# A two-layer decoder trunk: compression products over four column quarters, stick-breaking heads in pairs, heads alternating in the value products

## The chip, the cores and the metric

The kernel runs on one core of one Trainium2 chip. The metric is the device time of one launch in microseconds. A core has a matrix engine (PE in the profile, with its weight loads shown apart as PEld), a vector engine (DVE), a scalar engine (ACT), a third elementwise engine (POOL) and a queue engine (SP) that issues the DMAs of the weights.

## The reference, cut to what matters

Two layers, each `x + 0.5 SwiGLU`, then a mixer, then `x + 0.5 SwiGLU`. SEQ is 256, the model width 1024, all in float32. The mixer runs three attentions over one projection of the normed input and adds them with learned gates. The parts that the change touches:

```
# A, stick-breaking, 4 heads of 64: per head and block of 128 queries
z = q @ k.T / 8
log_1m = where(past, log_sigmoid(-z), 0)
tail = reversed exclusive cumsum of log_1m over keys
w = where(past, exp(log_sigmoid(z) + tail), 0);  o = w @ v
# B, NSA, 8 heads in 2 groups: o = g0*compressed + g1*selected + g2*window
nsa_compress: blocks of 32 tokens, stride 16 -> 15 blocks per group
    silu(flat(blocks + pe) @ w1) @ w2        # w1: 2048 x 128, w2: 128 x 64, for k and for v
# C, DSA, 4 heads: an indexer scores all keys, the top 64 are kept, softmax over them, times v
```

## The kernel before, in words

The weights (some 209 MB) stream through as tiles of 128x1024 (512 KB, four buffers). Each is split into a high part `wh` (line 244, ACT) and a low part `wl` (line 246, DVE, a few on POOL), and the products run as `wh` by the activations and `wl` by their high part. One such tile is a unit. Up to two units are split ahead of the one whose products run (`LA`).

The attention work of a mixer runs in threads (Python generators: `keys`, `indexer`, `queries`, `nsa_units`, `compress`, `stick_breaking`, `nsa`, `compressed`, `dsa`). After each unit, `tick` lets each thread go on to its next `yield n`, which means: be called again n units later. So the program order of PE is units with pieces of attention between them, and PE keeps exactly the written order (`pe` chains each instruction to the one before). The order on DVE, ACT and POOL is set by a tile scheduler from priorities and dependences, and within an engine it is fixed as well. Banks of PSUM are shared by tag: `acc` three, `sc` two, `tp` two, `o` one.

What the change touches:

- `compress` (lines 778 to 837). POOL writes `flat`, the 15 blocks of each group beside each other for k and v. Then four chunks of `w1` (one weight load of 512 KB each) with eight products: the 30 columns of `flat` are the stationary operand, 128 columns of `w1` stream, and all 16 products of k (or v) add up in 30 rows of bank `o`. A plain float32 product is two passes on PE, and the trace has a record for each. Then a sigmoid on 30x256 (exp on ACT, lines 799 to 801 on DVE), two transposes back, copies into `hrep` (line 613), a product with `w2`, a norm and a rotation of the compressed key (lines 816 to 828), `kc` (line 611 on ACT and line 675 on POOL), two transposes of it, and `kC`.
- `sb_head` (lines 1017 to 1046), one thread for each of the four heads, two units apart. Scores z into an `acc` bank, from 64 rows of `qT` and `kT` (a head is the upper or lower half of the 128 rows); Abs (line 1025), exp and ln (line 477) on ACT; line 1028 on DVE adds max(z, 0), line 1030 casts to the high part, line 1032 takes the low part; two units after z, four products with `tri` add the cumulated sum into the same bank; then exp to `w`, and the value products into 64 rows of a `tp` bank.
- `nsa_unit` (lines 963 to 979): the value products of two heads, one into the upper, one into the lower 64 rows of bank `o`: all of the one head, then all of the other. `dsa` (lines 905 on) does the like for four heads.

In names of the order listings, the number behind a name is the buffer's.

Of the kernel before, what the change touches and what calls it, by code (L numbers as in the profile page):

```python
# [17 lines left out]
P = 128  # L18
# [38 lines left out]
def _constants():  # L57
# [30 lines left out]
    put("csc", c)  # L88
    put("snc", s)
    put("rowmask", (r[:, None] // 16 == np.arange(8)[None, :]))  # L90
    cm = np.zeros((P, NT, 16))
# [19 lines left out]
HG = 2  # L111
WB = 4
WARM = 40
# [12 lines left out]
def decoder_trunk(ctx: ExitStack, tc: tile.TileContext, x_in, consts, gains, hgain, gu1, dn1, win, wkc, wgate, cw1, cw2,  # L126
# [339 lines left out]
    def mixer(l, nrm, nxt):  # L466
# [215 lines left out]
        def indexer():  # L682
# [22 lines left out]
            for t in range(NT):  # L705
# [6 lines left out]
                for h0 in range(0, 8, per):  # L712
                    sc = psum("sc", SC).rearrange("p (h k) -> p h k", k=nk)
                    for j in range(per):
                        mm(sc[:, j], iqS[:, h0 + j, t * P:(t + 1) * P], ikS[:, 0:nk], True, True)
                    rl = mt([512], "rl", 2).rearrange("p (h k) -> p h k", k=nk)
                    A.activation(out=rl, in_=sc, func=AF.Relu)
                    for j in range(per):
                        w = iw[:, t, h0 + j:h0 + j + 1]
                        if h0 + j == 0:  # L720
                            V.tensor_scalar(out=isc[t], in0=rl[:, j], scalar1=w, scalar2=None, op0=ALU.mult)
                        else:
                            V.scalar_tensor_tensor(out=isc[t], in0=rl[:, j], scalar=w, in1=isc[t], op0=ALU.mult,  # L723
                                                   op1=ALU.add)
                    if h0 % 4 == 0:
                        yield 1
# [47 lines left out]
        kC = mt([2, 32], "kC", 1, F32R)  # L774
        vpad = mt([8, HD], "vpad")

        def compress():
            yield from need("f")
            yield 2
            flat = b4("flat")[:, 0:64 * NC].rearrange("p (k j g c) -> p k j g c", k=2, j=16, g=2)  # L780
            for kv in range(2):
                for hf in range(2):
                    for g in range(2):
                        fv = fk[:, kv, g, 1:257].rearrange("p (c j e) -> p j c e", j=8, e=2)[:, :, hf:hf + NC, 0]
                        G.tensor_tensor(out=flat[:, kv, 8 * hf:8 * hf + 8, g], in0=fv,
                                        in1=pos[:, kv, 8 * hf:8 * hf + 8].unsqueeze(2).to_broadcast([P, 8, NC]), op=ALU.add)
            hid = psum("o", 1)
            for kv in range(2):
                for c in range(2):
                    w1 = load(cw1[l, kv][:, c * 1024:(c + 1) * 1024])  # L790
                    yield 1
                    for j in range(8):
                        jj = c * 8 + j
                        mm(hid[0:2 * NC, kv * P:(kv + 1) * P], flat[:, kv, jj].rearrange("p g c -> p (g c)"),
                           w1[:, j * P:(j + 1) * P], jj == 0, jj == 15)
            hs = mt([2, P], "kc4")[0:2 * NC]
            hv = hid[0:2 * NC, 0:2 * P].rearrange("p (a b) -> p a b", b=P)
            act_exp(out=hs, in_=hv, scale=-1.0)
            V.tensor_scalar(out=hs, in0=hs, scalar1=1.0, scalar2=None, op0=ALU.add)
            V.reciprocal(out=hs, in_=hs)  # L800
            V.tensor_tensor(out=hs, in0=hs, in1=hv, op=ALU.mult)
            hrep = mt([2, 4, 2, 16], "hrep")
            G.memset(hrep, 0.0)
            yield 2
            tp = psum("tp", TP)
            for kv in range(2):
                pe(T.transpose(tp[:, kv * 32:kv * 32 + 2 * NC], hs[:, kv], ident[0:2 * NC, 0:2 * NC]))
            for kv in range(2):
                evens(out=hrep[:, kv, :, :, 0:NC], in_=tp[:, kv * 32:kv * 32 + 2 * NC]
                              .rearrange("p (g c) -> p g c", c=NC).unsqueeze(1).to_broadcast([P, 4, 2, NC]))  # L810
            yield 2
            c2 = psum("o", 1)
            for kv in range(2):
# [17 lines left out]
            stack_k(kc4, kc.unsqueeze(1), 1)  # L831
            G.tensor_tensor(out=vpad, in0=c2s[:, 1].unsqueeze(1).to_broadcast([P, 8, HD]),
                            in1=cc("rowmask").unsqueeze(2).to_broadcast([P, 8, HD]), op=ALU.mult)
# [67 lines left out]
        def dsa():  # L901
            yield from need("mdsa", "qD")
            for t in range(NT):
# [12 lines left out]
                o = psum("tp", TP)  # L916
                for h in range(4):
                    for b in range(t + 1):
                        mm(o[h % 2 * HD:(h % 2 + 1) * HD, h // 2 * P:(h // 2 + 1) * P], vds[:, b], PT[h][b],
                           b == 0 and h < 2, True)  # L920
# [38 lines left out]
        def nsa_unit(t, i):  # L959
# [13 lines left out]
            yield from need(("o", t), 2)  # L973
            for a in range(2):
                for b in range(t + 1):
                    for j in range(2):
                        mm(ob[t][a * HD:(a + 1) * HD, i * P:(i + 1) * P], (vsel, vwin)[j][:, b, a], PT[2 * a + j][b], False,
                           True)
# [3 lines left out]
        def nsa():  # L982
            yield from need("PTc")
            for t in range(NT):
                ob[t] = o = psum("o", 1)
                for i in range(4):
                    mm(o[:, i * P:(i + 1) * P], vpad[:, 2 * i:2 * i + 2].rearrange("p a d -> p (a d)"),
                       PTc[:, t * P:(t + 1) * P], i == 0, True)
# [16 lines left out]
        def stick_breaking():  # L1005
# [5 lines left out]
            yield 1  # L1011
            for h in range(4):
                spawn(sb_head(h))
                yield 2

        def sb_head(h):
            i, a = h // 2, h % 2
            d = slice(a * HD, (a + 1) * HD)
            z = psum("acc", ACC)
            mm(z[:, 0:S], kT[d, i, 0:P], qT[d, i], True, False)  # L1020
            mm(z[:, S:S + P], kT[d, i, P:S], qT[d, i, P:S], False, False)
            mm(z[:, 0:512].rearrange("p (b q) -> p b q", b=2)[:, :, 0:P], negi, mstr, False, True)
            z = z[:, 0:S + P]
            sp = mt([512], "rl", 2)[:, 0:S + P]
            A.activation(out=sp, in_=z, func=AF.Abs)
            act_exp(out=sp, in_=sp, scale=-1.0)
            act_exp(out=sp, in_=sp, func=AF.Ln, bias=1.0)
            V.scalar_tensor_tensor(out=sp, in0=z, scalar=0.0, in1=sp, op0=ALU.max, op1=ALU.add)
            sh = mt([S + P], "w", WB, F32R)
            V.tensor_copy(out=sh, in_=sp)  # L1030
            sl = mt([S + P], "w", WB, F32R)
            V.tensor_tensor(out=sl, in0=sp, in1=sh.bitcast(F32), op=ALU.subtract)
            yield 2
            for v in (sh, sl):
                mm(z, tri[:, 0], v, False, False)
            for v in (sh, sl):
                mm(z[:, P:S], tri[:, 1], v[:, S:S + P], False, v is sl)
            yield 2
            w = mt([S + P], "w", WB)
            act_exp(out=w, in_=z)  # L1040
            yield 1
            o = psum("tp", TP)
            mm(o[d, 0:S], vsb[:, 0, h * HD:(h + 1) * HD], w[:, 0:S], True, False)
            mm(o[d, P:S], vsb[:, 1, h * HD:(h + 1) * HD], w[:, S:S + P], False, True)
            A.activation(out=OT[0][d, i], in_=o[d, 0:S], func=AF.Copy)
            V.tensor_tensor(out=OT[1][d, i], in0=o[d, 0:S], in1=OT[0][d, i].bitcast(F32), op=ALU.subtract)

# [165 lines left out]
```

## Time and profile before

| | us |
|---|---|
| median of 3 runs (lowest, highest) | 1254.26 (1252.81, 1255.97) |
| the profiled execution | 1254.2 |
| its span in the trace | 1252.2 |
| mean granted clock of PE | 0.993 of full |
| PE busy, share of the span | 1231.1 (98%) |
| DVE busy | 906.6 (72%) |
| ACT busy | 696.9 (56%) |
| POOL busy | 168.8 (13%) |

The profile's page first lists the busy time of each engine. Then comes the chain of work that ended last: from the last instruction back, at each step to what released it, with the share of the span that each engine has in it. A timeline row has the start in us, the duration in us, the engine, the line, the operation, the tiles written and read, the shape, and how many instructions of one kind the row holds; in brackets the idle time ahead of it and what ended that. Matmuls are pipelined, so two neighbouring rows of PE overlap: what a piece of work costs is read from its start to the next row's start. A layer's mixer lies at 206 to 446 us in the first layer and at 820 to 1066 us in the second.

### The profile page before, as it was taken

Reading aid. Unit: us, or ns where it says so; the run is one execution under the profiler, and the core shown is the slowest. Engines: PE = TensorE matmul, PEld = TensorE weight load, DVE = VectorE, ACT = ScalarE, POOL = GpSimd, SP = SyncE. Lnnn points to the kernel's source line nnn. Section 1 sums busy time; section 2 is a strip of 40 time slices with the busy share of each in tenths; the row PEclk is TensorE's granted clock in tenths of the full one; section 3 lists DMA queues with packets and bytes.
Section 4 is the critical chain, followed back from the end, with each engine's and each line's share of the span. In section 5 each row is a group of like instructions: output and inputs, shape, how many; then the busy total and the mean of one; then the engine's idle time right before and its main releaser. Section 6 shows DMA issues by size and latency. Waiting matters only on the chain.

```text
span 1252.2 us, 20870 instructions
## 1 busy us (share of the span) xinstructions
PE 1231.1 (98%) x7868; PEld 1096.9 (88%) x7868; DVE 906.6 (72%) x1592; ACT 696.9 (56%) x1261; POOL 168.8 (13%) x193
## 2 busy tenths in 40 slices
PE   8999999989999999999999999999899999999998
PEld 7888888878999988888888888888798999888887
DVE  6777677898675976666776666779977668777654
ACT  6655554545665565555555555545556745555542
POOL 2211011220001121110111110131200012111100
PEclk8999999989999999999999999999999999999999
DMA  6655565543333565555655555665333345555563
GB/s 232 192 193 188 184 186 188 192 134 110 127 102 118 175 195 186 185 182 184 189 179 192 186 181 185 190 192 187 119 119 109 118 141 183 179 193 191 180 201 107
DMA packets 61171, 212.05 MB, mean 169 GB/s; under 512 B 7024, under 2 KB 8592, under 8 KB 61072
## 3 DMA queue, kind: packets, MB, share of 16 engines
q1 hardware_dynamic: 60480, 209.63, 52.2%
q0 software_dynamic: 448, 1.08, 0.4%
q8 instruction: 61, 1.00, 0.3%
q14 instruction: 38, 0.31, 0.1%
q10 hardware_dynamic: 144, 0.02, 0.0%
HBM read 209.14 MB, written 1.05 MB: 168 GB/s over the span
## 4 chain that ended last, share of the span: by engine, by line
PE 89%; DVE 7%; ACT 1%; issue 1%; DMA 1%; POOL 1%; SPq 0%; DVEq 0%; POOLq 0%; ACTq 0%
PE acc L195 68%; PE sc L195 16%; PE o L195 2%; DVE wl L246 2%; PE tp L664 2%; PE tp L195 1%; ACT wh L244 1%; DVE isc L733 1%; DMA x<-in_x 1%; DVE isc L723 0%; DVE m L732 0%; DMA hg<-in_hgain 0%; POOL v L422 0%; DVE kc L800 0%; POOL kc L675 0%
## 5 line engine op out<-in xcount | busy, mean ns | idle before, releaser
L244 ACT ACTIVATE wh<-raw 128x1024 fp32r<-128x1024 f32 (+3 forms) x405 | 412.2, 1021 | 452.1 <-PE acc L195 309.1
L246 DVE TENSOR_TENSOR wl<-raw,wh 128x1024 fp32r<-128x1024 f32 (+3 forms) x397 | 469.0, 1184 | 244.1 <-ACT wh L244 242.7
L195 PE MATMUL acc<-aT,wh 128*128 128x512 f32 (+1 forms) x1696 | 462.3, 344 | 2.6 <-DVE aT L356 2.6
L195 PE MATMUL acc<-aT,wl 128*128 128x256 f32 x1280 | 361.0, 282 | 0.2 <-DVE wl L246 0.2
L195 PEld LDWEIGHTS acc<-aT,wh 128*128 128x128 f32 x1696 | 292.8, 190 | 45.2 <-DVE aT L356 3.9
L195 PE MATMUL acc<-hT,wh 128*128 128x512 f32 (+1 forms) x792 | 247.9, 369 | 0.0
L195 PEld LDWEIGHTS acc<-aT,wl 128*128 128x128 f32 x1280 | 243.9, 191 | 1.1 <-DVE wl L246 1.0
L195 PE MATMUL acc<-hT,wl 128*128 128x256 f32 x704 | 199.1, 283 | 0.0
L195 PE MATMUL sc<-aT,wh 128*128 128x512 f32 x544 | 192.4, 396 | 0.0
L195 PEld LDWEIGHTS acc<-hT,wh 128*128 128x128 f32 x792 | 142.8, 188 | 26.9
L195 PE MATMUL sc<-aT,wl 128*128 128x256 f32 x544 | 152.5, 280 | 0.6 <-DVE wl L246 0.6
L195 PEld LDWEIGHTS acc<-hT,wl 128*128 128x128 f32 x704 | 132.4, 188 | 0.0
L422 POOL TENSOR_TENSOR v<-v,R 128x256 f32<-128x256 f32 x88 | 69.7, 796 | 415.5 <-DVE v L338 362.9
L195 PEld LDWEIGHTS sc<-aT,wh 128*128 128x128 f32 x544 | 102.0, 188 | 23.8
L195 PE MATMUL acc<-wh,aT 128*128 128x512 f32 (+1 forms) x320 | 108.4, 405 | 0.0
L195 PEld LDWEIGHTS sc<-aT,wl 128*128 128x128 f32 x544 | 102.7, 189 | 0.9 <-DVE wl L246 0.9
L195 PEld LDWEIGHTS acc<-wh,aT 128*128 128x128 f32 x320 | 62.4, 195 | 12.2 <-issue 0.4
L366 POOL TENSOR_TENSOR ssum<-ssum,sq 128x256 f32<-128x256 f32 x42 | 39.4, 938 | 194.5 <-ACT sq L365 194.1
L195 PE MATMUL acc<-wl,aT 128*128 128x512 f32 (+1 forms) x160 | 63.2, 395 | 0.0
L246 POOL TENSOR_TENSOR wl<-raw,wh 128x1024 fp32r<-128x1024 f32 x8 | 19.6, 2452 | 269.6 <-ACT wh L244 269.6
L337 ACT ACTIVATE half<-acc 128x256 f32<-128x256 f32 x136 | 49.4, 365 | 2.6 <-PE acc L195 1.2
L424 DVE TENSOR_TENSOR v<-v,v 128x256 f32<-128x256 f32 x88 | 38.3, 437 | 13.1 <-ACT v L423 5.1
(242 smaller groups left out, 1444.8 us busy)
## 6 DMA issues: line engine op xcount, KB each, us to landing
raw<-in_gu SPq DMA_DIRECT2D x175, 512.0 KB, 4.1
raw<-in_dn SPq DMA_DIRECT2D x64, 512.0 KB, 3.6
raw<-in_wgate SPq DMA_DIRECT2D x48, 512.0 KB, 3.3
raw<-in_win SPq DMA_DIRECT2D x32, 512.0 KB, 3.3
raw<-in_dn SPq DMA_DIRECT2D x32, 384.0 KB, 3.0
raw<-in_wbr SPq DMA_DIRECT2D x16, 512.0 KB, 3.5
raw<-in_wout SPq DMA_DIRECT2D x16, 512.0 KB, 3.4
raw<-in_cw SPq DMA_DIRECT2D x8, 512.0 KB, 4.1
```

Of the source, the lines that this page charges most:

```text
L195: return pe(T.matmul(o, lhsT=lhsT, rhs=rhs, start=start, stop=stop, skip_group_check=True))
L244: A.activation(out=wh[:, w], in_=raw[:, w], func=AF.Copy)
L246: e.tensor_tensor(out=wl[:, w], in0=raw[:, w], in1=wh[:, w].bitcast(F32), op=ALU.subtract)
L337: A.activation(out=t, in_=b[:, S:2 * S], func=AF.Copy)
L366: G.tensor_tensor(out=ssum, in0=ssum, in1=sq, op=ALU.add)
L422: G.tensor_tensor(out=g, in0=g, in1=N["R"], op=ALU.mult)
L424: V.tensor_tensor(out=u, in0=u, in1=g, op=ALU.mult)
L664: pe(T.transpose(tp[:, b * P:(b + 1) * P], src, ident))
L733: V.match_replace(out=isc[t], in_to_replace=m8, in_values=isc[t], imm_value=MARK)
```

## The change: what it does

Three edits.

1. Compression. The 16 products of k (and of v) no longer add up in one place. Each goes to one of four column quarters, 32 wide (30 columns and two spare ones), so product j adds to rows 32·(j mod 4) of the bank. The four sums are then copied by ACT (`hq`), and one product for k and one for v with a constant matrix of zeros and ones ("quarters") adds the four and transposes them at once; they stand where the two transposes stood. The sigmoid is then taken on 128x60 instead of 30x256, and two DVE products write `hrep`. The `yield 2` there becomes a `yield 1`, so the rest of the compression is one unit earlier.
2. Stick-breaking. One thread for two heads, five units apart. The products of z and of o alternate between the two heads (two halves of the rows, two halves of the columns); elementwise work runs on tiles of [2, 384] where it can.
3. In the value products of `nsa_unit` and `dsa` the heads alternate inside the blocks.

The diff, cut to its core:

```diff
@@ compress
-                        mm(hid[0:2 * NC, kv * P:(kv + 1) * P], flat[:, kv, jj].rearrange("p g c -> p (g c)"),
-                           w1[:, j * P:(j + 1) * P], jj == 0, jj == 15)
-            hs = mt([2, P], "kc4")[0:2 * NC]
-            hv = hid[0:2 * NC, 0:2 * P].rearrange("p (a b) -> p a b", b=P)
-            act_exp(out=hs, in_=hv, scale=-1.0)
+                        f0 = (kv * 16 + jj) * 2 * NC
+                        mm(hid[jj % 4 * 32:(jj % 4 + 1) * 32, kv * P:(kv + 1) * P], fl[:, f0:f0 + 32],
+                           w1[:, j * P:(j + 1) * P], jj < 4, jj >= 12)
+            hq = mt([2, P], "kc4")
+            A.activation(out=hq, in_=hid[:, 0:2 * P].rearrange("p (a b) -> p a b", b=P), func=AF.Copy)
+            hrep = mt([2, 4, 2, 16], "hrep")
+            G.memset(hrep, 0.0)
+            yield 1
+            tp = psum("tp", TP)
+            for kv in range(2):
+                mm(tp[:, kv * 2 * NC:(kv + 1) * 2 * NC], hq[:, kv], cc("quarters"), True, True)
+            hs = mt([4 * NC], "hs4")
+            act_exp(out=hs, in_=tp[:, 0:4 * NC], scale=-1.0)
             V.tensor_scalar(out=hs, in0=hs, scalar1=1.0, scalar2=None, op0=ALU.add)
             V.reciprocal(out=hs, in_=hs)
-            V.tensor_tensor(out=hs, in0=hs, in1=hv, op=ALU.mult)
-            hrep = mt([2, 4, 2, 16], "hrep")
-            G.memset(hrep, 0.0)
-            yield 2
-            tp = psum("tp", TP)
             for kv in range(2):
-                pe(T.transpose(tp[:, kv * 32:kv * 32 + 2 * NC], hs[:, kv], ident[0:2 * NC, 0:2 * NC]))
-            for kv in range(2):
-                evens(out=hrep[:, kv, :, :, 0:NC], in_=tp[:, kv * 32:kv * 32 + 2 * NC]
-                              .rearrange("p (g c) -> p g c", c=NC).unsqueeze(1).to_broadcast([P, 4, 2, NC]))
+                a, b = (v[:, kv * 2 * NC:(kv + 1) * 2 * NC].rearrange("p (g c) -> p g c", c=NC).unsqueeze(1)
+                        .to_broadcast([P, 4, 2, NC]) for v in (hs, tp))
+                V.tensor_tensor(out=hrep[:, kv, :, :, 0:NC], in0=b, in1=a, op=ALU.mult)
             yield 2
...
@@ dsa
-                for h in range(4):
-                    for b in range(t + 1):
+                for b in range(t + 1):
+                    for h in range(4):
@@ nsa_unit
-            for a in range(2):
-                for b in range(t + 1):
-                    for j in range(2):
+            for b in range(t + 1):
+                for j in range(2):
+                    for a in range(2):
@@ stick_breaking
-            for h in range(4):
-                spawn(sb_head(h))
-                yield 2
+            for i in range(2):
+                spawn(sb_pair(i))
+                yield 5
+        def sb_pair(i):
+            halves_ = [slice(a * HD, (a + 1) * HD) for a in range(2)]
+            zs = [psum("acc", ACC) for _ in range(2)]
+            for z, d in zip(zs, halves_):
+                mm(z[:, 0:S], kT[d, i, 0:P], qT[d, i], True, False)
+            for z, d in zip(zs, halves_):
+                mm(z[:, S:S + P], kT[d, i, P:S], qT[d, i, P:S], False, False)
...
+            for a in range(2):
+                A.activation(out=sp[:, a], in_=zs[a], func=AF.Abs)
             act_exp(out=sp, in_=sp, scale=-1.0)
             act_exp(out=sp, in_=sp, func=AF.Ln, bias=1.0)
+            for a in range(2):
+                V.scalar_tensor_tensor(out=sp[:, a], in0=zs[a], scalar=0.0, in1=sp[:, a], op0=ALU.max, op1=ALU.add)
+            sh = mt([2, S + P], "w", WB, F32R)
             V.tensor_copy(out=sh, in_=sp)
+            sl = mt([2, S + P], "w", WB, F32R)
             V.tensor_tensor(out=sl, in0=sp, in1=sh.bitcast(F32), op=ALU.subtract)
             yield 2
             for v in (sh, sl):
+                for a in range(2):
+                    mm(zs[a], tri[:, 0], v[:, a], False, False)
...
+            for a in range(2):
+                mm(o[halves_[a], 0:S], v(a, 0), w[:, a, 0:S], True, False)
+            for a in range(2):
+                mm(o[halves_[a], P:S], v(a, 1), w[:, a, S:S + P], False, True)
```

Beside this, `vpad` shares the buffer of `p1`, the tile `rl` is [2, 384] wide, and `w` of stick-breaking lies in it.

How the instructions move. First PE at the scores of stick-breaking in the first layer, before (one head):

```order
L195 MATMUL acc_3442<-qT_2171,kT_2170 128x256
L195 MATMUL acc_3442<-qT_2171,kT_2170 128x128
L195 LDWEIGHTS negi
L195 MATMUL acc_3442<-mstr,negi 128x2x128
L195 MATMUL acc_3461<-aT_132,wh_3330 128x256 x2
```

and after (two heads, in the banks 3444 and 3445):

```order
L196 MATMUL acc_3444<-qT_2170,kT_2169 128x256
L196 MATMUL acc_3445<-qT_2170,kT_2169 128x256
L196 MATMUL acc_3444<-qT_2170,kT_2169 128x128
L196 MATMUL acc_3445<-qT_2170,kT_2169 128x128
L196 LDWEIGHTS negi
L196 MATMUL acc_3444<-mstr,negi 128x2x128
L196 LDWEIGHTS negi
L196 MATMUL acc_3445<-mstr,negi 128x2x128
L196 MATMUL acc_3469<-aT_132,wh_3332 128x256 x2
```

The second head's scores stood two units later before; they now stand between those of the first.

PE at the end of the compression in the first layer, before: `dq` are transposes of another thread, `kc` the compressed key, and the `acc` rows one unit's twelve products of 512 columns.

```order
L664 MATMUL tp_2973<-cst,dq_2870 128x128 x4
L195 MATMUL acc_2959<-wh_2900,aT_132 128x512
L195 MATMUL acc_2959<-wl_2901,aT_132 128x512
L195 MATMUL acc_2959<-wh_2900,aT_132 128x512 x2
L195 MATMUL acc_2959<-wl_2901,aT_132 128x512
L195 MATMUL acc_2959<-wh_2900,aT_132 128x512
L195 MATMUL acc_2960<-wh_2900,aT_132 128x512
L195 MATMUL acc_2960<-wl_2901,aT_132 128x512
L195 MATMUL acc_2960<-wh_2900,aT_132 128x512 x2
L195 MATMUL acc_2960<-wl_2901,aT_132 128x512
L195 MATMUL acc_2960<-wh_2900,aT_132 128x512
L664 MATMUL tp_3021<-cst,kc_577_2949 128x128 x2
```

and after:

```order
L665 MATMUL tp_2975<-cst,dq_2887 128x128 x4
L665 MATMUL tp_2989<-cst,kc_569_2899 128x128 x2
L196 MATMUL acc_2961<-wh_2906,aT_132 128x512
L196 MATMUL acc_2961<-wl_2907,aT_132 128x512
L196 MATMUL acc_2961<-wh_2906,aT_132 128x512 x2
L196 MATMUL acc_2961<-wl_2907,aT_132 128x512
L196 MATMUL acc_2961<-wh_2906,aT_132 128x512
```

The transposes of the compressed key stand one unit (twelve products) earlier.

DVE at the end of the compression in the first layer, before: `c2s` is the compressed key before its transposes, `q`, `ra` and `rb` belong to the query thread, and `m` to the top 64 of the indexer.

```order
L637 SCALAR_TENSOR_TENSOR w_2884<-w_2884,u_2882 128x1
L626 TENSOR_TENSOR rb_2980<-q_402_2154,cst 128x8x8
L638 SCALAR_TENSOR_TENSOR y_2883<-w_2884,y_2883 128x1
L732 MAX m_589_3005<-isc_2377 128x8
L823 SCALAR_TENSOR_TENSOR c2s_2818<-c2s_2818,y_2883,hg_2140 128x64
L628 TENSOR_TENSOR q_402_2154<-ra_2979,rb_2980 128x8x16
L825 TENSOR_TENSOR cra_2892<-c2s_2818,cst 128x16
L826 TENSOR_TENSOR crb_2893<-c2s_2818,cst 128x8
L827 TENSOR_TENSOR crb_2893<-c2s_2818,cst 128x8
L844 CAST q_402_2154<-q_402_2154 128x8x64
L828 TENSOR_TENSOR c2s_2818<-cra_2892,crb_2893 128x16
L246 TENSOR_TENSOR wl_2990<-raw_2987,wh_2989 128x1024
```

and after:

```order
L831 SCALAR_TENSOR_TENSOR c2s_2783<-c2s_2783,y_2825,hg_2140 128x64
L734 MATCH_REPLACE isc_2377<-m_577_2947,isc_2376 128x128
L833 TENSOR_TENSOR cra_2834<-c2s_2783,cst 128x16
L834 TENSOR_TENSOR crb_2835<-c2s_2783,cst 128x8
L835 TENSOR_TENSOR crb_2835<-c2s_2783,cst 128x8
L601 TENSOR_TENSOR gl_2621<-acc_2846,R_2335 128x512
L836 TENSOR_TENSOR c2s_2783<-cra_2834,crb_2835 128x16
L734 MATCH_REPLACE isc_2377<-m_578_2950,isc_2377 128x256
L637 TENSOR_TENSOR w_2892<-y_2891 128x8
L247 TENSOR_TENSOR wl_2958<-raw_2955,wh_2957 128x1024
L638 SCALAR_TENSOR_TENSOR w_2892<-w_2892,u_2890 128x8
L733 MAX m_591_3011<-isc_2376 128x8
```

The whole query chain (its scale, its gain, its rotation and the cast) and one `wl` stood ahead of the last `c2s` and now stand behind it.

## Rows read from the trace of the kernel before

**Rows 1.** The page: busy time by engine, and the chain that ended last.

```profile
PE 1231.1 (98%) x7868; PEld 1096.9 (88%) x7868; DVE 906.6 (72%) x1592; ACT 696.9 (56%) x1261; POOL 168.8 (13%) x193
...
PE 89%; DVE 7%; ACT 1%; issue 1%; DMA 1%; POOL 1%; SPq 0%; DVEq 0%; POOLq 0%; ACTq 0%
```

**Rows 2.** Windows: window, length; busy of PE, PEld, DVE, ACT, POOL; clock; DMA.

```profile
236.00:282.00 46.00, 41.64 (x239) 35.25 (x238) 42.76 (x108) 22.13 (x39) 10.62 (x9) 0.93 0.45 148
...
312.00:397.00 85.00, 85.00 (x695) 78.30 (x695) 53.00 (x102) 54.79 (x118) 2.36 (x1) 1.00 0.38 120
275.00:281.00 6.00, 5.41 (x14) 4.26 (x15) 4.71 (x17) 0.23 (x1) 0.53 (x1) 0.50 0.42 126
```

**Rows 3.** Timeline of PE at one chunk of the compression.

```profile
225.88 1.93 PE L195 MATMUL o<-raw,flat 128*30 128x128 f32 x16
227.75 0.47 PE L195 MATMUL acc<-wh,aT 128*128 128x448 f32 x1
```

**Rows 4.** Timeline of PE: NSA value products, first block of queries, one unit.

```profile
329.21 0.45 PE L195 MATMUL o<-PT,vsel 128*64 128x128 f32 x4
329.48 0.40 PE L195 MATMUL o<-PT,vwin 128*64 128x128 f32 x4
329.80 0.66 PE L664 MATMUL tp<-cst,E 128*128 128x128 f32 x4
```

**Rows 5.** The same, second block of queries, two units (first and last row).

```profile
383.63 0.43 PE L195 MATMUL o<-PT,vsel 128*64 128x128 f32 x2
...
386.13 0.87 PE L664 MATMUL tp<-cst,E 128*128 128x128 f32 x6
```

**Rows 6.** Timeline of PE: scores, sums and values of stick-breaking heads.

```profile
312.80 0.92 PE L195 MATMUL acc<-qT,kT 64*128 64x256 f32 x4
313.65 0.28 PE L195 MATMUL acc<-mstr,negi 128*128 128x256 bf16 x1
...
320.98 0.77 PE L195 MATMUL acc<-w,tri 128*128 128x384 f32 x4
...
335.57 0.86 PE L195 MATMUL tp<-w,vsb 128*64 128x256 f32 x4
336.37 0.50 PE L195 MATMUL acc<-aT,wh 128*128 128x256 f32 x2
```

**Rows 7.** Timelines of ACT and DVE: from that head's scores to its sums.

```profile
313.97 0.49 ACT L1025 ACTIVATE rl<-acc 128x384 f32<-128x384 f32 x1 [0.20 <-PE acc L195]
...
315.72 1.10 ACT L477 ACTIVATE rl<-rl 128x384 f32<-128x384 f32 x2
...
317.08 0.55 DVE L1028 SCALAR_TENSOR_TENSOR rl<-acc,rl 128x384 f32<-128x384 f32 x1
317.67 0.36 DVE L1030 CAST w<-rl 128x384 fp32r<-128x384 f32 x1
...
319.08 0.55 DVE L1032 TENSOR_TENSOR w<-rl,w 128x384 fp32r<-128x384 f32 x1
```

**Rows 8.** Timelines of DVE and PE from the compression's sigmoid to its transposes.

```profile
233.66 1.23 DVE L246 TENSOR_TENSOR wl<-raw,wh 128x1024 fp32r<-128x1024 f32 x1 [0.45 <-ACT wh L244]
...
245.40 1.38 DVE L799 TENSOR_SCALAR kc<-kc 30x256 f32<-30x256 f32 x1
246.81 1.74 DVE L800 RECIPROCAL kc<-kc 30x256 f32<-30x256 f32 x1
...
268.53 0.68 DVE L652 TENSOR_TENSOR q<-q,y 128x512 f32<-128x512 f32 x1
...
272.98 0.42 DVE L844 CAST q<-q 128x512 fp32r<-128x512 f32 x1
273.31 0.17 DVE L828 TENSOR_TENSOR c2s<-cra,crb 128x16 f32<-128x16 f32 x1
...
273.88 0.33 PE L664 MATMUL tp<-cst,kc 128*128 128x128 f32 x1 [1.42 <-ACT kc L611]
275.59 0.47 PE L664 MATMUL tp<-cst,kc 128*128 128x128 f32 x1 [1.38 <-POOL kc L675]
```

## What the change should do to the time

> **What bounds the kernel now.** The first view is the page: PE is busy for 98% of the span and makes 89% of the chain that ended last [rows 1]. So a microsecond that PE no longer works is a microsecond of the span, unless PE then waits for something that was hidden. The second view, busy time by windows, says where that danger is [rows 2]. From 312 to 397 us, where stick-breaking and NSA run, PE is busy for 85.00 of 85.00 us and the others for at most 65% of it: a saving goes straight into the time there. From 236 to 282 us, where the compressed key is made, PE is busy for only 41.64 of 46.00 and DVE for 42.76: the vector engine is nearly full and PE waits for it. The third view, the timelines, gives the price of each piece from its start to the next row's start.
>
> **Compression products.** A chunk of eight products is 16 passes on PE and takes 227.75 − 225.88 = 1.87 us, 0.117 a pass [rows 3]. How four quarters run, this trace does not show; two halves it does: the eight passes of an NSA unit, four to the upper and four to the lower half, take 329.80 − 329.21 = 0.59 us [rows 4], as much as five of the passes above, that is four places and 0.12 of entry and exit. If four quarters share places as two halves do, 16 passes need four places, so 0.59 as well: 1.28 less a chunk, four chunks a layer, 5.1 us a layer. The two products with the constant matrix stand for two transposes; they cost at most two passes more, 0.2. PE alone would gain 4.9 us a layer.
>
> Whether it does is decided by DVE. Its work from the `wl` at 233.66 to the last `c2s` at 273.31 + 0.17 = 273.48 is 39.8 us with hardly a hole [rows 8, 2]. Out go the addition and the reciprocal on 30x256, 1.38 + 1.74 = 3.1; in come the same on 128x60, by 60 of 256 elements in a row 0.7 (an estimate from these two rows). The product and the copy into `hrep` become two products of a like size: nothing. By the order of DVE the query chain and one `wl` no longer stand ahead of the last `c2s`: two multiplications of 0.68, a cast of 0.42 and a `wl` of 1.23 make 3.0 [rows 8], beside smaller ones (the rotation, a MAX and a replacement), about 1 in all. DVE would be done at 273.5 − 3.1 + 0.7 − 3.0 = 268.1, or 267.1 with the small ones. From there to the second transpose it is 275.59 − 273.48 = 2.1 us, most of it POOL's half of `kc`, as before. So the transposes can run at 269.2 to 270.2.
>
> PE was there at 273.88 − 1.42 = 272.5 and waited 1.42 + 1.38 = 2.8 us for both halves of `kc` [rows 8]. Now it is there 4.9 earlier, and one unit of twelve products earlier, since the transposes moved ahead of it. A product of 512 columns takes 6.00 / 14 = 0.43 at a granted clock of 0.50 (the lower of the two levels, 1.2 GHz, that PE had after this wait) [rows 2], so 0.21 at the full one, and twelve 2.6. PE arrives at 265.0 and waits 4 to 5 us: the wait grows. Behind the transposes are now these twelve products. The slow clock after a wait costs half of six microseconds, some 2.7 of the 5.41 busy ones, in both kernels alike. At the same point of the program PE is then ahead by 275.6 − (270.2 + 2.6) = 2.8 us by the large operations alone, 3.8 with the small ones; above stands PE's own 4.9. I take 3.9, the middle of 2.8 and 4.9, and the same in the second layer, whose mixer has the same program: **7.8 us**, with 5.6 and 9.8 as ends. The other limit on the first step, that PE looks ahead over only some passes and so fills fewer than four quarters at a time, lies within these ends, since DVE swallows it first.
>
> **Values of stick-breaking.** One head's products into 64 rows take 336.37 − 335.57 = 0.80 us [rows 6]. Two heads alternate between the halves that rows 4 show running together, so the second costs almost nothing: 0.80 for each of four pairs, **3.2 us**. The gap ahead of such a stretch is not counted; it would come on top.
>
> **Scores.** A head's z from 64 rows takes 313.65 − 312.80 = 0.85 [rows 6]. No row shows two halves of the rows together. If they share places as columns do, 0.85 × 4 = 3.4. If not, two heads need twelve places of 0.117 = 1.4 instead of 1.7, 1.2 in all. I take **3.0**, near the upper end, since the halves of columns [rows 4] are the nearest thing that was measured.
>
> **NSA values.** In the second block of queries two units have 32 passes and take 386.13 − 383.63 = 2.50 us [rows 5]. The heads stand one behind the other there, and the second gets in only when the first is nearly through. Alternating, 16 places of 0.117 and 0.12 make 1.99: 0.51 less, four such stretches (two a layer), **2.0 us**. The first block (0.59 for eight passes) is at four places already and gains nothing; nor does the DSA loop, whose halves alternated before.
>
> *A rule against this reading.* Rows 4 show the four passes with `vsel` of both heads ahead of the last ones with `vwin`, though the program has the first head's `vwin` before the second head's `vsel`. The Trainium skill (TensorE: Matmul & The Clock Gate, Part 3, The mechanism) says that matmuls start and end strictly in program order, without reordering. By that rule the alternation would also help the first block, and the quarters would fill more slowly, which is rival E below; the trace speaks against it.
>
> **The wait added.** A pair's chain is ACT and DVE work between z and the product with `tri`. For one head it is 0.49 + 1.10 + 0.55 + 0.36 + 0.55 = 3.05 us of work and ran from 313.97 to 319.63 among other work, while PE came to `tri` only at 320.98 [rows 7, 6]. For a pair the work is at most 6.1, so without any overlap it ends at 322.7, 1.7 late. Behind the waiting product on PE stand all units that follow, so a wait there is paid in full. But Abs of one head runs beside the exp of others, the double tiles save starts, and PE begins with the high parts (more than 0.77 us for the four products of one head), so that the low part is needed last. Between 0 and 1.7 I take 0.4 for the first pair of a layer, which has the softmax of NSA on ACT beside it, and nothing for the second: **−0.8**. The third `acc` bank is left to the units during a pair; no row of PE shows a wait for a bank in 312 to 397 [rows 2], and I price it at nothing.
>
> **Sum.** 7.8 + 3.2 + 3.0 + 2.0 − 0.8 = 15.2 us. The profiled execution took 1254.2, the median of the runs is 1254.26, so no correction is needed: 1254.2 − 15.2 = **1239.0 us**. With the ends of each term (5.6 to 9.8, 1.2 to 3.4, stalls 0 to 3.4) it goes from 1234 to 1243.6.
>
> **Rivals.**
>
> A: the compression gains nothing. DVE is full, and what PE saves becomes a longer wait for `kc`; or the four quarters run one after the other and the change does not do what it says there. For it: 42.76 of 46 us [rows 2]. Against it: the order moves 3 us of DVE work behind the key. Time: 1239.0 + 7.8 = 1246.8.
>
> E: products run side by side only in the order of the program. The second pass of a product needs the same place as its first, so the eight products of a chunk need nine places, 1.17 us instead of 0.59: 0.58 × 8 = 4.6, of which the share that reaches the end above (7.8 of 10.3) is 3.5. A pair's values and scores need five places for four: 0.20 × 4 + 0.21 × 4 = 1.6. Time: 1239.0 + 5.1 = 1244.1. Rows 4 speak against it.
>
> B: the chain of DVE gets ahead of PE. Then the wait of 2.8 and the slow clock (2.7) vanish and PE's own 4.9 comes whole: 10.4 a layer, 20.8 instead of 7.8: 1226.0. For it: two DVE operations less and a shorter chain. Against it: DVE would have to be 4 to 5 us faster still.
>
> D, slower: the pair's chain holds PE. If the second head's 3.05 us comes wholly on the path at each of the four pairs, and the clock falls after each wait as it did after 275 us (2.7), that is 5.75 × 4 = 23.0, and with the 0.8 counted already 1239.0 + 22.2 = 1261.2. It decides from 4.0 us a pair (16.0 / 4), where it eats all gains. For it: PE came to `tri` only 1.35 us after the chain's end [rows 6, 7]. Against it: ACT has 54.79 and DVE 53.00 busy in 85 us [rows 2].
>
> **Chances.** Forecast 0.60, A 0.16, E 0.07, B 0.10, D 0.04, others 0.03. About 0.3%, 3.8 us, is what can be told from no change. Forecast, B, A and E are faster by more, less 0.03 for tails of A: 0.90. Within it 0.05 (those tails, half of the others), slower 0.05 (D, the rest). The forecast's own range is 1234 to 1244; down to 1229 and up to 1248 it takes in A and E and leaves out B and D.
>
> **What would show it.** Right: the 16 passes of a chunk take about 0.6 us; a pair's values about 0.8 and its scores 0.85 to 1.4; two NSA units in the second block 2.0; PE still waits for `kc`, 4 to 5 us now, and the wait for `tri` stays below 1 us. A: chunk as short, but the wait for `kc` 7 us or more. E: a chunk of 1.2. B: no wait for `kc` and no window of clock 0.50 behind it. D: waits of PE for `w` of 3 us at the pairs. The forecast is wrong where the chunk is short and a new wait of more than 1 us stands at another place in the mixers.

## The result and the profile after

The changed kernel takes 1231.55 us (median of 4 runs, 1230.66 to 1234.24) against 1254.55 (4 runs, 1252.81 to 1255.97): a ratio of 0.982, 95% interval 0.980 to 0.9839. 1239.0 was forecast, with 1229 to 1248 as range. So the direction held, and the gain of 23 us is half as large again as the 15.2 of the sum. The stated range held only at its wide lower end: 1231.55 lies below the forecast's own 1234 to 1244. One of the nine runs of `sig_act_before` took 1488.27 us at a mean granted clock of 0.752 and is left out of its figures below.

The page of the changed kernel answers to [rows 1]; its execution took 1230.66 us, with a span of 1227.8:

```profile
PE 1204.7 (98%) x7872; PEld 1076.2 (88%) x7872; DVE 895.1 (73%) x1580; ACT 694.1 (57%) x1249; POOL 173.1 (14%) x195
...
PE 86%; DVE 9%; DMA 2%; issue 1%; ACT 1%; SPq 0%; POOL 0%; DVEq 0%; ACTq 0%; POOLq 0%
```

PE has 26.4 us less to do, and its share of the span is what it was. The next rows are the timeline of PE in the changed kernel, first layer; they answer to [rows 3 to 6]:

```profile
239.45 0.65 PE L196 MATMUL o<-raw,flat 128*32 128x128 f32 x16
240.02 0.50 PE L196 MATMUL acc<-wh,aT 128*128 128x512 f32 x1
...
323.31 0.44 PE L196 MATMUL o<-PT,vsel 128*64 128x128 f32 x4
323.58 0.39 PE L196 MATMUL o<-PT,vwin 128*64 128x128 f32 x4
323.90 0.66 PE L665 MATMUL tp<-cst,E 128*128 128x128 f32 x4
...
328.06 0.87 PE L196 MATMUL tp<-rl,vsb 128*64 128x256 f32 x8
328.86 0.92 PE L196 MATMUL acc<-qT,kT 64*128 64x256 f32 x8
329.72 0.39 PE L196 MATMUL acc<-mstr,negi 128*128 128x256 bf16 x2
...
374.72 0.44 PE L196 MATMUL o<-PT,vsel 128*64 128x128 f32 x4
...
376.62 0.55 PE L665 MATMUL tp<-cst,E 128*128 128x128 f32 x3
```

From start to next start: a chunk 0.57 us (it was 1.87), two heads' values 0.80 (0.80 for one), two heads' scores 0.86 (0.85 for one), two NSA units of the second block 1.90 (2.50), the unit of the first block 0.59 as before. By these prices the sixteen passes over four quarters take the time of about four places, and halves of the rows run together as halves of the columns do.

Where the time went is read from three places of each layer's mixer that both programs have. The kernel before, timeline of PE:

```profile
225.88 1.93 PE L195 MATMUL o<-raw,flat 128*30 128x128 f32 x16
283.96 0.28 PE L195 MATMUL sc<-mdsa,negi 128*128 128x256 bf16 x1
396.27 0.39 PE L195 MATMUL acc<-iqS,wh 128*128 128x256 f32 x1
846.16 1.93 PE L195 MATMUL o<-raw,flat 128*30 128x128 f32 x16
903.10 0.28 PE L195 MATMUL sc<-mdsa,negi 128*128 128x256 bf16 x1
1015.41 0.39 PE L195 MATMUL acc<-iqS,wh 128*128 128x256 f32 x1
```

and the changed one:

```profile
227.85 0.64 PE L196 MATMUL o<-raw,flat 128*32 128x128 f32 x16
278.32 0.28 PE L196 MATMUL sc<-mdsa,negi 128*128 128x256 bf16 x1
386.48 0.38 PE L196 MATMUL acc<-iqS,wh 128*128 128x256 f32 x1
832.50 0.64 PE L196 MATMUL o<-raw,flat 128*32 128x128 f32 x16
882.95 0.28 PE L196 MATMUL sc<-mdsa,negi 128*128 128x256 bf16 x1
991.09 0.39 PE L196 MATMUL acc<-iqS,wh 128*128 128x256 f32 x1
```

From the first chunk to the indexer's mask the stage took 58.08 and takes 50.47 in the first layer, 56.94 and 50.45 in the second: 7.6 and 6.5 us, **14.1** where 7.8 was forecast. From there to the projection the stick-breaking and NSA stage took 112.31 and takes 108.16, then 112.31 and 108.14: 4.2 us a layer, **8.3** where 7.4 was forecast. Together 22.4. The spans differ by 24.4; the other 2.0 lie in stages that the change does not touch (last section).

The first of these two is where the forecast was off. PE's waits in the first layer's mixer, kernel before, then changed kernel (total, times, longest):

```profile
PE tp L664 <- ACT kc L611: 1.4, 1, 1.4
PE tp L664 <- POOL kc L675: 1.4, 1, 1.4
PE tp L664 <- DVE hrep L613: 0.9, 1, 0.9
...
PE tp L664 <- ACT kSW L759: 0.6, 1, 0.6
```

```profile
PE tp L665 <- ACT wh L245: 1.5, 1, 1.5
PE tp L665 <- ACT qD L770: 1.5, 1, 1.5
PE tp L665 <- POOL kc L676: 0.8, 1, 0.8
...
PE tp L665 <- ACT PT L901: 0.7, 1, 0.7
PE tp L665 <- ACT kSW L760: 0.6, 1, 0.6
```

In the stage of the key 4.3 us of waits before and 4.4 after. (The releasers of the first two are by the profile's last event. The first one ends as DVE has read the `tp` bank into `hrep`, 251.47 + 0.27; the second stands at the transposes of `kc`.) What differs is the clock, in the rows (as [rows 2]) behind the key's transposes, changed kernel, both layers:

```profile
270.00:276.00 6.00, 6.00 (x27) 4.99 (x28) 6.00 (x20) 1.67 (x4) 1.57 (x1) 1.00 0.59 173
876.00:882.00 6.00, 6.00 (x28) 4.99 (x27) 6.00 (x18) 2.12 (x2) 1.58 (x1) 1.00 0.48 158
```

Before, it was 0.50 for six us in the first layer [rows 2] and for three in the second (896 to 899 us, also 0.50). This is one execution of each kernel, and they stand far apart: the mean granted clock of the profiled executions is 0.993 and 0.999, while 48 other runs of the kernel before that list it have 0.992 to 1.000, 0.9962 on the mean, and the changed kernel's other three runs 0.997, 0.995 and 0.997.

### The profile page after: what moved, and what is told of

It is laid out like the page before. It is cut to its first block, busy times and chain, and to the rows that moved or that the text cites. A ratio compares the mean times of both kernels' runs of the same rounds, so it can differ in the third digit from the quotient of the medians.

```text
span 1227.8 us, 20844 instructions
## 1 busy us (share of the span) xinstructions
PE 1204.7 (98%) x7872; PEld 1076.2 (88%) x7872; DVE 895.1 (73%) x1580; ACT 694.1 (57%) x1249; POOL 173.1 (14%) x195
## 4 chain that ended last, share of the span: by engine, by line
PE 86%; DVE 9%; DMA 2%; issue 1%; ACT 1%; SPq 0%; POOL 0%; DVEq 0%; ACTq 0%; POOLq 0%
PE acc L196 65%; PE sc L196 16%; DVE wl L247 4%; PE tp L665 2%; PE o L196 2%; DMA raw<-in_win 1%; PE tp L196 1%; ACT wh L245 1%; DVE isc L734 1%; DVE m L733 1%; DVE isc L724 1%; DMA x<-in_x 1%; DMA hg<-in_hgain 0%; POOL ssum L367 0%; DVE q L656 0%
## 5 line engine op out<-in xcount | busy, mean ns | idle before, releaser
L196 PE MATMUL acc<-wh,aT 128*128 128x512 f32 (+1 forms) x320 | 104.4, 392 | 0.0
```

Source lines behind the costliest of these rows:

```text
L196: return pe(T.matmul(o, lhsT=lhsT, rhs=rhs, start=start, stop=stop, skip_group_check=True))
```

## The experiments

Theory T, read from the two traces: PE's own saving comes through whole in the compression, and the slow clock behind the key is gone as well. Rival R: that stage gives 7.8 as forecast, and the rest comes from the pairs or from the edits acting together. The ratios are to the kernel before on the same chip.

**Each edit alone.** `p1_compress`, `p2_pairs` and `p3_alternate` are the kernel before with one of the three edits of the diff each.

> The kernel before with the compression edit alone. Theory T (read from the two traces): the compression stage gains PE's own 4.9 us a layer in full and the slow clock behind the wait for kc is gone (2.8 us in the first layer, 1.4 in the second), 13.9 us in all: 1254.5 - 13.9 = 1240.6, no window of clock 0.50 near 270 to 282 us. Rival R (the term as forecast, 7.8 us, the rest of the gain comes from the pairs and the heads alternating, or from the edits together): 1246.8, with a window of clock 0.50 left.

Measured: 1239.89 us, ratio 0.9886 (0.9868 to 0.9903), 14.3 us faster (12.2 to 16.6). T's number holds, R's does not. A chunk takes 0.57 and the waits are those of the changed kernel to 0.1 us in the first layer. One thing that T said did not hold: in the second layer a window of 0.50 is left (3 us from 877 on), made good there by a wait for `hrep` of 0.5 instead of 1.5. And over the runs the clock hardly differs: 0.9966 on the mean of these five, 0.9962 for the kernel before on the same chip. So the number speaks for T, but not for its clock.

> The kernel before with stick-breaking by pairs alone (vpad in the buffer of p1, as the pairs' wider tiles need the room). Theory T: two heads' values 0.80 instead of about 1.7 and two heads' scores 0.86 instead of about 1.8, four pairs, less the new waits for PT (0.7 a layer): 6 to 7 us faster, 1248. Rival R: with 23 us in all and 7.8 from compression, some 13 us: 1241.5.

Measured: 1247.78, ratio 0.9951 (0.9936 to 0.9965), 6.1 us faster (4.4 to 8.0): T. In its trace the stick-breaking and NSA stage takes 110.61 and 109.09 us instead of 112.31; the first layer has some 3 us at 0.50 from 296 on, behind a wait of 0.35.

> The kernel before with the alternating heads in the value products of NSA and DSA alone. Theory T and the forecast: 2.0 us faster, 1252.5, two units of the second block 2.0 us instead of 2.50, the first block unchanged at 0.59. Rival E (strict order of the program): 3.5 us more, 1249, since then the first block would gain as well.

Measured: 1250.85, ratio 0.9969 (0.9954 to 0.9984), 3.9 us faster (2.0 to 5.8): the forecast's 2.0 is at the interval's edge. In its trace the same stage takes 111.34 and 111.36, so 1.9 in all. The first block's unit still takes 0.59, so at this distance the order of the program does not hold matmuls back. The three alone sum to 24.3, the three together give 23: within the intervals they add up. In the traces, 3.2 (the pairs, second layer) and 1.0 make the 4.2 a layer of the changed kernel.

**The places side by side.** The changed kernel with another order of the quarters:

```diff
-  mm(hid[jj % 4 * 32:(jj % 4 + 1) * 32, ...], ..., jj < 4, jj >= 12)
+  mm(hid[jj // 4 * 32:(jj // 4 + 1) * 32, ...], ..., jj % 4 == 0, jj % 4 == 3)
```

> The changed kernel with the same four quarters, but four products after each other go to one quarter (j div 4 in place of j mod 4): same instructions, other order of places. If PE looks ahead over a few passes only (four, as two NSA units behind each other suggest), a chunk takes 12 places, 1.4 to 1.5 us instead of 0.57; strictly in the order of the program 15 places, 1.8; freely reordered 0.6 to 1.1. Of 0.9 us x 4 = 3.6 us a layer PE arrives later at the key's transposes, where it waits 2.2 us: theory T (PE and DVE nearly tie there) expects 1.4 us a layer lost, 1234.5; a stage bound by DVE alone 1231.5 to 1232; one bound by PE alone 1238.8.

Measured: 1238.1, ratio 0.9875 (0.986 to 0.989), that is 6.5 us slower than the changed kernel by the medians. Timeline of PE in this kernel:

```profile
240.21 1.53 PE L196 MATMUL o<-raw,flat 128*32 128x128 f32 x16
241.67 0.50 PE L196 MATMUL acc<-wh,aT 128*128 128x512 f32 x1
```

A chunk takes 1.46 us: about 12 places of 0.117, so by this count the second quarter starts when four passes of the first are left. What counts is that products to different quarters follow each other closely. T's number for the total (1234.5) missed: of 0.89 × 8 = 7.1 us that PE works longer, shorter waits absorb about 2 (0.5 instead of 1.5 us a layer for `hrep`), the wait for `kc` stays (2.1 instead of 2.2), and three us at a clock of 0.50 in the second layer add 1.5: 6.6. That it is so near the 1238.8 of a stage bound by PE is in part this clock: in the first layer, without it, the stage takes 52.76 instead of 50.47, so 2.3 of the 3.6 us come through. DVE's last `c2s`, changed kernel and this one:

```profile
267.80 0.17 DVE L836 TENSOR_TENSOR c2s<-cra,crb 128x16 f32<-128x16 f32 x1
268.23 0.16 DVE L836 TENSOR_TENSOR c2s<-cra,crb 128x16 f32<-128x16 f32 x1
```

Counted from the first chunk (227.85, and 225.96 here), it ends at 40.1 and at 42.4. So DVE's end does not stand at a fixed time behind the first chunk, as in the forecast's picture: PE works 3.6 us longer, and DVE's end moves by 2.3 of them.

**One unit earlier.** The changed kernel with the old `yield 2` (`y2`), and the kernel before with `yield 1` and nothing else (`y1_before`).

> The changed kernel with the yield of 2 back in the compression (all that follows the four sums is one unit later, as before the change). Theory P (DVE follows PE: its chain begins when PE has finished the chunks, and PE's saving comes through): PE waits less for hrep (1.5 us a layer at most) and the key's transposes stand one unit later, so the end moves by at most that: 1229 to 1233. Rival Y (putting it one unit earlier is what took away the slow clock and 3 us of work ahead of the key): the waits for kc are 2.8 again, a window of clock 0.50 is back in both layers, 1231.5 + 3 to 4 = 1235.

Measured: 1231.91, ratio 0.983 (0.9807 to 0.9853), as the changed kernel. The key's transposes wait for nothing now, but PE waits 4.8 us in the stage of the first layer (4.3 in the second) at other transposes:

```profile
PE tp L665 <- ACT kSW L760: 4.8, 3, 2.7
```

Rival Y is half right here: the wait for `kc` is not back, but in this trace the clock of 0.50 is, in both layers, for some 3 us behind the longest of these waits. Second layer (as [rows 2]):

```profile
867.00:868.00 1.00, 1.00 (x6) 1.00 (x6) 1.00 (x3) 0.35 (x2) 0.00 (x0) 0.50 0.32 57
868.00:869.00 1.00, 1.00 (x7) 1.00 (x6) 1.00 (x6) 0.00 (x0) 0.00 (x0) 0.50 0.84 291
```

Here the quarters stand without the unit earlier, and the median is the changed kernel's all the same.

> The kernel before with the one unit earlier alone (yield 1 for yield 2 behind the compression's sums; products and sigmoid as before). Rival Y: 3 to 4 us faster, 1250.5, no clock of 0.50. Theory P: the wait for hrep grows from 0.9 to 2 or 3 us a layer, since the sigmoid on 30x256 is as slow as it was; the key comes earlier by less than a unit; 1252.5 to 1256.

Measured: 1248.66, ratio 0.9965 (0.9948 to 0.9982), 4.4 us faster (2.3 to 6.5). Here rival Y is right in the time and P fails, though the wait that P expected came (2.4 us for the sigmoid, line 801). The trace has no wait for `kc`, 3.8 us of waits at other places (those 2.4 among them) and no slow clock in either layer. So in the kernel before, one number in the schedule was worth 4 us. In the traces that is 0.5 us of waits a layer, and 2.7 and 1.5 us of clock in the two layers (half of the busy time at 0.50). But the profiled run (1244.62, clock 0.999) is one of the fastest of the twelve; over the runs the mean clock is 0.9968 against 0.9958 for the kernel before on this chip, some 1.3 us. What makes up the rest of the 4.4 is not shown.

**The key made late.** The changed kernel, with ACT copying the high part of the key over itself n more times:

```diff
             evens(out=d[:, :, 0:2].bitcast(F32R), in_=b)
+            for _ in range(again):   # 4 or 12, for the compressed key only
+                A.activation(out=d[:, :, 0:2].bitcast(F32R), in_=d[:, :, 0:2].bitcast(F32R), func=AF.Copy)
```

> The changed kernel with ACT copying the high part of the compressed key four more times over itself before POOL takes the low part (the values stay the same): the key comes 4 x 0.31 = 1.2 us later or more. Theory P (PE waits there, so it is paid in full): 1.2 to 2 us a layer, 1234 to 1236, and a longer wait at kc. If the key had slack, nothing. Clock theory: with a wait as long as before's (2.8 us) the clock falls to 0.50 in some layers, another 1.4 us each.

Measured: 1233.79, ratio 0.9846 (0.982 to 0.9871). PE waits 2.73 + 0.21 in the first layer and 2.7 in the second, where it waited 1.46 + 0.78: 0.7 and 0.4 us more, less than expected, as POOL's half followed sooner. The clock behind it, first and second layer:

```profile
268.00:274.00 6.00, 6.00 (x28) 4.96 (x28) 6.00 (x20) 2.18 (x5) 1.24 (x1) 1.00 0.49 165
874.00:880.00 6.00, 5.67 (x14) 4.32 (x15) 6.00 (x19) 1.76 (x4) 1.69 (x2) 0.50 0.55 170
```

The same wait, and the clock fell once and once not: half the products in the same time (14 for 28).

> The same with twelve more copies: 3.7 us later or more in each layer. Theory P: 1231.5 + 7.4 to 12 = 1239 to 1243.5, plus 1.4 to 2.8 us a layer if the clock falls to 0.50 after a wait of 5 to 6 us, as it did in the kernel before after 2.8; if length of wait is not what makes it fall, the clock stays at 1.00 in at least one layer.

Measured: 1242.61, ratio 0.9922 (0.9897 to 0.9947). PE waits 6.56 + 0.27 us in both layers, and the clock is at 0.50 behind both. By the ratios it is 12.8 us slower than the changed kernel: 4.6 us more of wait a layer are 9.2, the other 3.6 fit the clock. The key has no slack: PE pays for its delay.

**DVE relieved.** In both kernels the sigmoid's addition and reciprocal move from DVE to ACT.

```diff
-            V.tensor_scalar(out=hs, in0=hs, scalar1=1.0, scalar2=None, op0=ALU.add)
-            V.reciprocal(out=hs, in_=hs)
+            act_exp(out=hs, in_=hs, func=AF.Ln, bias=1.0)
+            act_exp(out=hs, in_=hs, scale=-1.0)
```

> The kernel before with the sigmoid of the compression on ACT alone: exp of minus the log of 1 + exp(-x), in place of the addition and the reciprocal on DVE (3.1 us of DVE a layer). PE's order and work are the same. If DVE sets the end of the stage on its own (the forecast's step): the waits for kc of 2.8 us and the clock of 0.50 behind them go, 3 to 4.3 us a layer, 1244.5 to 1247. If PE's waits in the stage only move to another place and the clock alone is gained (as one unit earlier showed): 1.5 a layer, 1250. If DVE's time does not count there: 1253.

Measured: 1251.0, ratio 0.9973 (0.9961 to 0.9985), 3.4 us faster (1.9 to 4.9). DVE has 3.1 us a layer less to do, and its last `c2s` ends 46.0 us behind the first chunk instead of 47.6. The wait for `hrep` and the first wait for `kc` are gone, 2.8 us of waits are left of 4.3, and the clock stays at 1.00 in both layers. So the time is nearest to the second expectation (1250), but the waits did not merely move: 1.5 us a layer of them went, half of what DVE was relieved of.

> The changed kernel with the same edit, on 128x60 (the addition of 1.27 us and the reciprocal of 0.52 leave DVE). If DVE sets the end: the wait for hrep (1.5 us) and part of that for kc go, 1.5 to 1.8 us a layer, 1228 to 1228.5. If the waits only move: 1231.5.

Measured: 1234.4, ratio 0.9838 (0.9819 to 0.9857). Not faster than the changed kernel: in the first layer the wait for `hrep` goes (1.5; 0.6 of it stays in the second), the one for `kc` grows from 2.2 to 2.8, and 0.6 for `kSW` comes.

> The same with the yield of 2 back. In y2 PE waited 4.8 us a layer, all of it for kSW, the product of the key thread, which stands behind the sigmoid on DVE. If DVE sets the end: 1.8 us a layer, 1228.5; if not: 1231.9.

Measured: 1234.41, ratio 0.9842 (0.983 to 0.9855): no gain either, 2.9 us of wait for `hrep` and 1.4 for `kc`, with the clock at 0.50 for some 3 us behind the former in the first layer. No version run here beats the changed kernel.

## Why the prediction was right in direction and too small

**Held.** The prices of the side-by-side places: 0.59 forecast for a chunk and 0.57 measured, 0.80 and 0.80 for a pair's values, 0.85 and 0.86 for its scores (the upper end, 3.4, was right, not the 3.0 taken), 1.99 and 1.90 for two NSA units. The terms of that stage, 7.4 together, gave 8.3. Rivals A, E and D did not come: the chunks' saving arrived, the order of the program was no bar, and PE never waited for a pair's chain. In the first pair DVE ended the low part at 315.83 us and PE had begun `tri` at 315.38 with the high part. The stall, 0.8 for both layers in the sum, came at another place and larger: 0.7 us a layer for `PT` on ACT, behind the pair's value products. `p2_pairs` has that wait and the kernel before has not.

**Luck.** The forecast's ends were added up wrongly: its terms go from 1235.8 to 1245.6, not from 1234 to 1243.6. The measured 1231.55 lies below either, between the forecast and rival B (1226.0). It is inside the stated range because that was stretched down to 1229, for which the prediction names no mechanism: A and E, which the stretch was said to take in, are slower than the forecast. The compression's 14.1 lies above the term's upper end of 9.8.

**The steps that failed.** Both stand in the compression's term, forecast 7.8 and measured 14.1 in the traces, 14.3 by `p1_compress`.

1. "Whether it does is decided by DVE": the forecast let DVE's work run on from a `wl` at a fixed 233.66 us, took out what the edit removes, and so got 5.4 to 6.4 us for the last `c2s`, 3.9 of PE's 4.9 us a layer and 4 to 5 us of wait for `kc`. Counted from the first chunk, as all that follows, the last `c2s` ended at 47.6 and ends at 40.1: 7.5 earlier, and the wait is 2.2. What the order of DVE gives was right: one unit earlier alone (`y1_before`), which in its trace puts the query chain behind the key, brings it to 43.7, so 3.9 us, where 3.0 to 4.0 were forecast. The quarters alone (`y2`) leave that chain ahead of the key and bring it to 43.8 in the first layer, so 3.8 us, where the forecast had 2.4 from the shorter sigmoid. That sigmoid is only 1.3 us shorter (1.27 + 0.52 instead of 3.12; the estimate of 0.7 was too low), so some 2.5 us are work that starts earlier because PE is through with the chunks earlier: at 12.2 instead of 17.4. DVE's end hung in part on when PE fed it.

   In the changed kernel the waits of the stage sum to 4.4 us, as before (4.3), and PE's saving came whole: 4 × 1.30 = 5.2, less what the two products with the constant matrix cost more than the transposes (at most 0.2). That is 5.0 a layer, **10.0**. `q_serial` shows the same from the other side. (Not to be read as DVE counting for nothing: `sig_act_before` took 1.5 us of waits a layer away. No run has the quarters with the long sigmoid, so whether the saving would come whole without the 1.3 us is not shown.)
2. "The slow clock after a wait costs half of six microseconds ... in both kernels alike." It did not come in this stage of the changed kernel's profile. In this pair of traces that is worth 2.7 us in the first layer (half of 5.41 [rows 2]) and 1.5 in the second (half of three), **4.2**, of which the forecast had counted nothing. It was in rival B, but tied there to the end of all waiting, and that tie was wrong: 4.4 us of waits remained and the clock did not fall.

10.0 + 4.2 = 14.2 against 14.1 measured in the traces. But the 4.2 belong to this pair of executions. In the traces of `p2_pairs` and `p3_alternate`, whose compression is that of the kernel before, the stage takes 56.8 to 56.9 us in each layer, with a fall of the clock to 0.50 in each, so against them the changed kernel gains 12.6 to 12.8. And by the mean granted clocks, 0.9962 over 48 runs and 0.9970 over the changed kernel's four, the two kernels lose 4.7 and 3.7 us to the clock: 1 us apart. (A run's loss is what its mean clock lacks to 1, times its span; the slow clock at the start of the program counts in it.) So over the runs "in both kernels alike" was nearer than the traces say. What else fills `p1_compress`'s 14.3 (12.2 to 16.6) beyond 10.0 and such a clock is open.

What tells the waits with such a fall behind them from those without is not settled. A wait for `kc` of 2.6 to 2.8 us in two parts had one in both layers of the kernel before, of `p2_pairs` and of `p3_alternate`, and none in either layer of `sig_act`; 2.1 us had one in the second layer of `q_serial` and of `p1_compress`, and the changed kernel's 2.2 none in either; 2.7 to 2.9 had one in the second layer of `kc_late4` and none in the first. Behind 6.8 us it came both times. In the changed kernel it does not stay away for good: by their mean clocks its other three runs lost 2 to 5 us more than the profiled one, in places that are not on record.

## What to carry to other kernels

Small products that use a quarter or a half of the array are worth placing so that neighbours in the program go to different parts: here PE ran them at about the price of one as long as the next part was within a few passes, and not when four products to one part stood in a row (0.57 and 1.46 us a chunk). Where an engine looks full beside a waiting PE, ask what starts its work: if it starts at PE's own result, PE's saving moves it too, and the wait need not grow by all that PE saves. And price the clock behind a wait as a thing of its own, one that comes and goes with small moves in the schedule and from one execution to the next: read it from the granted clock of many runs, not from one pair of traces.

## What the runs showed of the hardware that was not expected

PE's rate in the FFN stages, which no edit touches, has two values, at a granted clock of 1.00 and without a wait in both. Matmuls in 80 us, from 50 and from 470 on, kernel before:

```profile
50.00:130.00 80.00, 80.00 (x463) 70.54 (x462) 56.40 (x87) 47.87 (x88) 10.74 (x15) 1.00 0.60 193
470.00:550.00 80.00, 80.00 (x455) 69.36 (x454) 54.77 (x85) 46.52 (x85) 10.37 (x14) 1.00 0.58 185
```

and the changed kernel:

```profile
50.00:130.00 80.00, 80.00 (x455) 69.36 (x454) 55.28 (x87) 46.29 (x86) 11.25 (x15) 1.00 0.63 190
470.00:550.00 80.00, 80.00 (x463) 69.98 (x462) 55.87 (x88) 47.02 (x87) 10.35 (x14) 1.00 0.65 190
```

463 or 455, 1.8% apart, and each of the four such stretches (from 50, 470, 660 and 1090 on) of all 13 traces has the one or the other to one matmul: `sig_act_before`, with the same FFN code, had 455 in all four. A stage gains or loses 2 us by it: from the projection of the first layer to the first chunk of the second, which holds two of them, it is 446.0 us with both at the higher rate (the changed kernel), 447.6 to 448.0 with one and 449.8 to 450.5 with none (the kernel before). Four stages make 8 us, so this and the clock can account for the 2 to 9 us over which runs of one kernel spread here; the rates of runs without a trace are not on record. The two profiled spans differ by 24.4 where the mixers account for 22.4: the stretch between the mixers gave 3.9, the first stage took 2.0 back. The cause of the two rates was not tried.
